# A gated MLP on one core: x transposed in bf16 groups inside five row chunks, gate and up weights read once per chunk, w_down loaded during the first stage

## The chip, the cores and the metric

One core of one Trainium2 chip. The metric is the device time of one execution in microseconds (us). "TensorE" is PE in the profile, "VectorE" DVE, "ScalarE" ACT, "GpSimd" POOL, "SyncE" SP. PSUM holds the tiles that TensorE writes to. PEld is the loading of a matmul's weights on TensorE. The granted clock (PEclk in the windows) is the share of its full clock that the profile shows for TensorE.

## The reference

```python
batch, seq_len, hidden_dim = 8, 1024, 1024        # M = 8192 rows, H = 1024
intermediate_dim = 4 * hidden_dim                 # I = 4096
def reference(x, w_gate, w_up, w_down):           # all float32
    gate = x @ w_gate
    up = x @ w_up
    gate = 0.5 * gate * (1 + np.tanh(np.sqrt(2 / np.pi) * (gate + 0.044715 * gate ** 3)))
    h = gate * up
    return (h @ w_down).astype(np.float32)
```

## The kernel before

The first stage transposes all of x with TensorE, then walks through 32 blocks of 128 columns of the gate and up weights; each block meets all 8192 rows, 512 at a time. The product h goes to DRAM. The second stage loads w_down and multiplies h by it. The lines that the argument touches:

```python
ident = const.tile([P, P], F32)
# --- first stage: P = 128, KH = 8, KI = 32, MT = 512
xt = xt_pool.tile([P, KH, M], BF16)                       # all of x, transposed: 128 KB a partition
for ms in range(NMS):                                     # 64 slices of 128 rows
    xs = stg.tile([P, H], F32, tag="xstage")
    nc.sync.dma_start(out=xs, in_=xf[ms * P:(ms + 1) * P, :])
    for ks in range(KH):
        pt = pst.tile([P, P], F32, tag="tp")              # two buffers
        nc.tensor.transpose(pt, xs[:, ks * P:(ks + 1) * P], ident)
        nc.vector.tensor_copy(out=xt[:, ks, ms * P:(ms + 1) * P], in_=pt)
for nb in range(KI):
    # ... wgf, wuf: 512 KB each by DMA; wgb, wub: their bf16 casts on GpSimd ...
    for mt in range(NMT):                                 # 16 row tiles of 512
        # ... 8 matmuls into gps, 8 into ups; gelu on ScalarE, product on VectorE, h to DRAM ...
# --- second stage, in pools of its own
wd = wd_pool.tile([P, KI, H], BF16)
for ko in range(KI):
    wdf = stg2.tile([P, H], F32, tag="wdf")               # two buffers
    nc.sync.dma_start(out=wdf, in_=wd_r[:, ko, :])
    nc.vector.tensor_copy(out=wd[:, ko, :], in_=wdf)
for mt in range(NMT):
    # ... hts: 4 MB of h; 8 accumulators (PSUM) of 32 matmuls each per tile, copied by ScalarE, written out ...
```

The program order is not the engine order: a scheduler interleaves the transposes with the first matmuls.

## Time and profile before

The median of the 13 runs of the kernel before is 2888.28 us; the span of the profiled run is 2886.6 us.

| stretch of the kernel before | time | its matmuls need | lost |
|---|---|---|---|
| first stage, to 1951.5 us | 1951.5 | 8192 x 215.83 ns = 1768.1 | 183 |
| second stage, to 2882.5 us | 931 | 4096 x 215.83 ns = 884.0 | 47 |
| tail | 4.1 | | 4 |

The spacing of 215.83 ns comes from the chain that ended last, in order of time (columns: start, length, what). One piece of the chain begins every 10.79 us and stands for 50 matmuls; one record in fifty is missing, so the line counts 49:

```profile
2066.07 10.74 PE ops L116 x49
2076.86 10.74 PE ops L116 x49
```

The page's chain shows how much of the span lies on TensorE:

```profile
PE 93%; DMA 3%; DVE 2%; issue 1%; SPq 0%; ACTq 0%; ACT 0%; DVEq 0%
```

The groups of instructions (columns: line, engine, operation, out<-in, shapes, count | busy us, mean ns of one | idle before, releaser) show the three kinds of matmul, the transposes (a matmul on L61) and their copies (L62):

```profile
L81 PE MATMUL gps<-xt,wgb 128*128 128x512 bf16 x4009 | 993.9, 384 | 4.2
...
L116 PE MATMUL ops<-wd,hts 128*128 128x512 bf16 x4014 | 887.1, 380 | 43.9 <-DVE wd L103 20.7
...
L61 PE MATMUL pt<-ident,xs 128*128 128x128 f32 x512 | 164.3, 358 | 46.7 <-DVE xt L62 28.3
...
L62 DVE CAST xt<-pt 128x128 bf16<-128x128 f32 x512 | 137.8, 290 | 90.0 <-PE pt L61 79.7
```

A matmul lasts 380 ns in its record, but a new one starts every 215.8 ns, as they overlap.

The stage windows (columns: window, its length, busy us and count of each engine, PEclk, DMA share, GB/s) show where the first stage loses its time:

```profile
50.00:100.00 50.00, 43.22 (x168) 22.77 (x170) 32.89 (x119) 1.79 (x3) 0.00 (x0) 0.76 0.48 160
100.00:150.00 50.00, 42.07 (x176) 21.79 (x176) 34.41 (x125) 2.39 (x4) 0.00 (x0) 0.84 0.51 168
240.00:300.00 60.00, 59.74 (x274) 27.20 (x278) 11.69 (x17) 10.75 (x18) 2.08 (x2) 1.00 0.24 74
```

From 50 to 150 us the granted clock is 0.76 to 0.84 and about 170 TensorE instructions, transposes among them, fit into 50 us; from 240 us on, 274 matmuls fit into 60.

### The profile page before, as it was taken

Reading aid. Unit: us, or ns where it says so; the run is one execution under the profiler, and the core shown is the slowest. Engines: PE = TensorE matmul, PEld = TensorE weight load, DVE = VectorE, ACT = ScalarE, POOL = GpSimd, SP = SyncE. Lnnn points to the kernel's source line nnn. Section 1 sums busy time; section 2 is a strip of 40 time slices with the busy share of each in tenths; the row PEclk is TensorE's granted clock in tenths of the full one; section 3 lists DMA queues with packets and bytes.
Section 4 is the critical chain, followed back from the end, with each engine's and each line's share of the span. In section 5 each row is a group of like instructions: output and inputs, shape, how many; then the busy total and the mean of one; then the engine's idle time right before and its main releaser. Section 6 shows DMA issues by size and latency. Waiting matters only on the chain.

```text
span 2886.6 us, 29837 instructions
## 1 busy us (share of the span) xinstructions
PE 2783.5 (96%) x12545; PEld 1278.0 (44%) x12800; DVE 510.7 (18%) x1056; ACT 381.2 (13%) x641; POOL 67.1 (2%) x70
## 2 busy tenths in 40 slices
PE   6889999999999999999999999995899999999999
PEld 3444444444444444444444444442344444444444
DVE  4663221112222222111222222111100000000000
ACT  0001111111111111111111111110000000000000
POOL 0000000000000000000000000000000000000000
PEclk8889999999999999999999999998999999999999
DMA  7452211211111121121121111118524224323321
GB/s 224 162 166 70 68 53 53 68 53 53 58 63 53 52 68 53 54 68 53 53 67 54 52 38 39 39 39 265 190 95 161 95 95 144 109 97 124 125 95 44
DMA packets 229254, 253.62 MB, mean 88 GB/s; under 512 B 12032, under 2 KB 208640, under 8 KB 229120
## 3 DMA queue, kind: packets, MB, share of 16 engines
q1 hardware_dynamic: 195840, 234.93, 24.3%
q10 hardware_dynamic: 33280, 16.78, 2.1%
q8 instruction: 100, 1.64, 0.2%
q14 instruction: 34, 0.28, 0.0%
HBM read 150.99 MB, written 100.66 MB: 87 GB/s over the span
## 4 chain that ended last, share of the span: by engine, by line
PE 93%; DMA 3%; DVE 2%; issue 1%; SPq 0%; ACTq 0%; ACT 0%; DVEq 0%
PE gps L81 31%; PE ups L84 30%; PE ops L116 29%; PE pt L61 3%; DMA wdf<-in_w_down_dram 3%; DVE xt L62 1%; DMA wuf<-in_w_up_dram 1%; SPq L102 0%; DVE wd L103 0%; DVE hsb L89 0%; DMA xs<-in_x_dram 0%; ACTq L73 0%; ACT osb L122 0%; SPq L90 0%; DVEq L89 0%
## 5 line engine op out<-in xcount | busy, mean ns | idle before, releaser
L81 PE MATMUL gps<-xt,wgb 128*128 128x512 bf16 x4009 | 993.9, 384 | 4.2
L84 PE MATMUL ups<-xt,wub 128*128 128x512 bf16 x4010 | 972.7, 379 | 4.2
L116 PE MATMUL ops<-wd,hts 128*128 128x512 bf16 x4014 | 887.1, 380 | 43.9 <-DVE wd L103 20.7
L116 PEld LDWEIGHTS <-hts 128*128 128x128 bf16 x4096 | 401.2, 98 | 529.7 <-issue 51.6
L81 PEld LDWEIGHTS <-wgb 128*128 128x128 bf16 x4096 | 407.0, 99 | 484.8 <-issue 15.0
L84 PEld LDWEIGHTS <-wub 128*128 128x128 bf16 x4096 | 404.3, 99 | 469.1
L89 DVE TENSOR_TENSOR hsb<-gsb,ups 128x512 bf16<-128x512 f32 x512 | 352.2, 688 | 1373.8 <-PE ups L84 1319.4
L87 ACT ACTIVATE gsb<-gps 128x512 f32<-128x512 f32 x512 | 305.7, 597 | 1623.5 <-PE gps L81 1553.6
L61 PE MATMUL pt<-ident,xs 128*128 128x128 f32 x512 | 164.3, 358 | 46.7 <-DVE xt L62 28.3
L122 ACT COPY osb<-ops 128x512 f32<-128x512 f32 x128 | 74.2, 588 | 858.5 <-PE ops L116 826.8
L62 DVE CAST xt<-pt 128x128 bf16<-128x128 f32 x512 | 137.8, 290 | 90.0 <-PE pt L61 79.7
L61 PEld LDWEIGHTS pt<-ident,xs 128*128 128x128 f32 x512 | 83.1, 163 | 120.4 <-DVE xt L62 93.4
L70 POOL CAST wgb<-wgf 128x1024 bf16<-128x1024 f32 x32 | 33.3, 1040 | 1692.2 <-PE gps L81 1475.3
L103 DVE CAST wd<-wdf 128x1024 bf16<-128x1024 f32 x32 | 22.2, 694 | 77.3 <-DMA wdf<-in_w_down_dram 77.3
L75 POOL CAST wub<-wuf 128x1024 bf16<-128x1024 f32 x32 | 33.3, 1040 | 27.0 <-PE ups L84 18.1
L87 ACT ACT_TABLE_LOAD x1 | 1.3, 1283 | 20.0 <-DMA wgf<-in_w_gate_dram 20.0
masks.py:199 POOL TENSOR_SCALAR_AFFINE_SELECT ident<-ident 128x128 f32<-128x128 f32 x1 | 0.3, 292 | 0.1
masks.py:197 POOL MEMSET ident<- 128x128 f32 x1 | 0.2, 204 | 0.3 <-POOLq L139 0.3
L139 POOL MEMSET const-float32-0.0<- 128x1 f32 x1 | 0.1, 98 | 0.2 <-issue 0.2
L139 POOL MEMSET const-bfloat16-1.0<- 128x1 bf16 x1 | 0.1, 102 | 0.0
L139 POOL MEMSET const-uint8-127<- 128x1 uint8 x1 | 0.1, 102 | 0.0
L139 POOL MEMSET const-float32-1.0<- 128x1 f32 x1 | 0.1, 98 | 0.0
## 6 DMA issues: line engine op xcount, KB each, us to landing
geglu_ht<-hsb SPq DMA_DIRECT2D x512, 128.0 KB, 1.7
hts<-geglu_ht SPq DMA_DIRECT2D x16, 4096.0 KB, 15.3
xs<-in_x_dram SPq DMA_DIRECT2D x64, 512.0 KB, 3.3
out_dram<-osb SPq DMA_DIRECT2D x64, 512.0 KB, 2.7
wuf<-in_w_up_dram ACTq DMA_DIRECT2D x32, 512.0 KB, 5.3
wgf<-in_w_gate_dram SPq DMA_DIRECT2D x32, 512.0 KB, 4.1
wdf<-in_w_down_dram SPq DMA_DIRECT2D x32, 512.0 KB, 4.2
```

Source lines behind the costliest of these rows:

```text
L61: nc.tensor.transpose(pt, xs[:, ks * P:(ks + 1) * P], ident)
L62: nc.vector.tensor_copy(out=xt[:, ks, ms * P:(ms + 1) * P], in_=pt)
L70: nc.gpsimd.tensor_copy(out=wgb, in_=wgf)
L75: nc.gpsimd.tensor_copy(out=wub, in_=wuf)
L81: nc.tensor.matmul(gps, wgb[:, ks, :], xt[:, ks, mt * MT:(mt + 1) * MT], start=(ks == 0), stop=(ks == KH - 1))
L84: nc.tensor.matmul(ups, wub[:, ks, :], xt[:, ks, mt * MT:(mt + 1) * MT], start=(ks == 0), stop=(ks == KH - 1))
L87: nc.scalar.activation(out=gsb, in_=gps, func=AF.Gelu_apprx_tanh)
L89: nc.vector.tensor_tensor(out=hsb, in0=gsb, in1=ups, op=mybir.AluOpType.mult)
L103: nc.vector.tensor_copy(out=wd[:, ko, :], in_=wdf)
L116: nc.tensor.matmul(ops, hts[:, ko, msub * P:(msub + 1) * P], wd[:, ko, dt * DT:(dt + 1) * DT], start=(ko == 0), stop=(ko == KI - 1),)
L122: nc.scalar.copy(out=osb[:, dt * DT:(dt + 1) * DT], in_=ops)
L139: nc = _bacc.Bacc("TRN2", target_bir_lowering=False, num_devices=1)
```

## The change

The intent: keep TensorE's matmuls dense from early on. x is transposed in bf16, eight 128x128 pieces to one PSUM tile with one VectorE copy; the rows are processed in five chunks, so that a chunk's transposes stand between matmuls of the chunk before; w_down is loaded during chunk 1, and the first tiles of h can be fetched before the first stage ends. The price: the gate and up weights are read five times.

```diff
+    wd = wd_pool.tile([P, KI, H], BF16)
+    def prep(xt, c, ms):
+        r0 = BASE[c] + ms * P
+        xs = stgx.tile([P, H], F32, tag="xstage", name="xs")
+        nc.sync.dma_start(out=xs, in_=xf[r0:r0 + P, :])
+        xb = stg.tile([P, H], BF16, tag="xstage_b", name="xb")
+        nc.gpsimd.tensor_copy(out=xb, in_=xs)
+        pt = pst.tile([P, KH, P], BF16, tag="tp", name="pt")
+        for ks in range(KH):
+            nc.tensor.transpose(pt[:, ks, :], xb[:, ks * P:(ks + 1) * P], ident)
+        nc.vector.tensor_copy(out=xt[:, :, ms * P:(ms + 1) * P], in_=pt)
+    CH = [1024, 2048, 2048, 2048, 1024]
+    for ms in range(CH[0] // P):
+        prep(xt_next, 0, ms)
+    for c in range(len(CH)):
+        xt = xt_next
         for nb in range(KI):
             # ... weights: loads and GpSimd casts as before, two staging buffers for three ...
+            if c == 1:
+                # ... wdf, one slice of w_down per block, cast on VectorE ...
-            for mt in range(NMT):
+            for mt in range(CH[c] // MT):
                 # ... matmuls as before; PSUM tiles gps and ups: two buffers for three ...
-                gsb = hp.tile([P, MT], F32, tag="gsb")
-                # ... gelu to gsb, product to hsb, one write of 512 columns ...
+                # ... gelu to hsb (bf16), product in place, two writes of 256 columns ...
+            if c + 1 < len(CH):
+                step = KI // (CH[c + 1] // P)
+                if nb % step == step - 1:
+                    prep(xt_next, c + 1, nb // step)
-    # ... second stage in its own pools: w_down loaded here, h in tiles of 512 rows, eight PSUM tiles ...
+    # ... second stage: h in tiles of 256 rows, two PSUM tiles, output written per 512 columns ...
```

## The prediction

> **What bounds it now.** TensorE. In the chain of waits, the second matmul stage advances by 10.79 us per 50 matmuls, 215.8 ns for each 512-column matmul, at granted clock 1.00. The Trainium skill ("TensorE: Matmul & The Clock Gate", Back-to-back issue gap) gives N/2.4 + 2.5 ns, 215.8 ns; the trace agrees. 12288 matmuls x 215.8 ns = 2652 us is a floor that the change doesn't touch. The span is 2886.6 us; 234.5 us is everything else. By the timeline and the stage windows:
> - The first stage ends at 1951.5 us, but its 8192 matmuls need 1768: **183 us** lost, nearly all before 240 us. There 512 fp32 transposes, each with its own PSUM tile and 290 ns VectorE copy, are interleaved singly with matmuls, the granted clock is 0.76 to 0.87, and the first matmul starts only at 26.4 us.
> - The second stage (1951.5 to 2882.5, 931 us) needs 884: **47 us** lost, where 32 weight slices (4.2 us to landing, then a 694 ns cast) are awaited.
> - Tail: 4 us.
>
> **What changes.**
> 1. Transposes: rows are cast to bf16 on GpSimd (about 1.04 us, as the weight casts there), eight bf16 transposes fill one PSUM tile, one VectorE copy empties it. By the instruction order, groups of eight stand between blocks of 64, 128 or 256 matmuls; only four groups precede the first matmul, eight the end of the start-up. The matmuls around them should keep the clock full. The 56 later groups stay on TensorE's path. Estimate: 0.9 us a group (the skill, same section, gives about 81 ns per sustained N=128 matmul; the trace's LDWEIGHTS is 98 ns, so about 100 ns a transpose, plus a switch), **50 us**.
> 2. Start-up: eight slices of x and two to four of each weight, at the 286 GB/s of the first 24 us, arrive by 20 to 25 us; minus 3.5 us of matmuls done meanwhile, **21 us** lost.
> 3. w_down is loaded and cast during chunk 1, and the first two tiles of h prefetched there: the 47 us go; **0 to 3 us** remain.
> 4. Added: the gate and up weights are read five times, 134 MB more. In the trace a 512 B packet takes 29.5 ns, 4 KB about 172 ns. Chunk 0 then needs weights 121 + h writes 30 + x 33 = 184 us of all 16 DMA engines in about 240 us: 77% busy. Weight loads run some two blocks (13.8 us) ahead and land in 4 to 5 us; so little waiting, **4 us** in all. Two instead of three PSUM buffers leave over 3 us of slack.
> 5. ScalarE and VectorE work per tile hardly changes and is off the path. Tail 4 us, launch 0.7.
>
> Sum: 2652 + 50 + 21 + 2 + 4 + 4 + 1 = 2734 us, 5.3% faster. Range 2712 to 2780. Chances: faster 0.95, same 0.04, slower 0.01.
>
> **What shows each step right or wrong.** The transposes' time per group of eight, about 0.9 us. Windows: clock near 1.00 after 30 us; chunk 0 (about 25 to 255 us) DMA share near 0.77, TensorE not waiting for GpSimd casts or weight DMAs. Timeline: first matmul about 18 us; no gap between stages; second stage about 884 us; matmul spacing still 215.8 ns.
>
> **What would make it wrong.** Transposes lowering the clock, or costing 150 ns or more each (+25 us); chunk 0 saturating the DMA engines, or in-order queues (weight loads in front of activations, casts in front of casts) making TensorE wait at block boundaries (+1 us per block would be +160 us).

## More of the kernel before

In the timeline of TensorE one sees the hand-over that slows the transposes: two small PSUM tiles go back and forth between TensorE and VectorE, and a pair takes 0.86 us (121.06 to 121.92).

```profile
121.06 0.69 PE L61 MATMUL pt<-ident,xs 128*128 128x128 f32 x2 [0.17 <-DVE xt L62]
121.92 0.69 PE L61 MATMUL pt<-ident,xs 128*128 128x128 f32 x2 [0.17 <-DVE xt L62]
```

## The result, and the profile after

The changed kernel takes 2709.31 us (median of 8 runs), the kernel before 2888.28 us. The ratio is 0.938, 95% interval 0.937 to 0.9389.

The direction and nearly all of the mechanism came as predicted, but 2709.3 lies 2.7 us below the range (2712 to 2780): the range missed.

The page after, groups of instructions and the chain:

```profile
PE 98%; DMA 1%; issue 1%; POOL 0%; SPq 0%; DVE 0%; ACT 0%; POOLq 0%; DVEq 0%; ACTq 0%
...
L112 PE MATMUL gps<-xt,wgb 128*128 128x512 bf16 x3999 | 961.9, 379 | 8.4 <-DVE xt L77 1.3
...
L76 PE MATMUL pt<-ident,xb 128*128 128x128 bf16 x512 | 41.2, 226 | 15.4 <-POOL xb L73 15.2
L76 PEld LDWEIGHTS <-xb 128*128 128x128 bf16 x512 | 35.2, 101 | 31.1 <-POOL xb L73 17.3
L77 DVE COPY xt<-pt 128x1024 bf16<-128x1024 bf16 x64 | 43.8, 685 | 22.5 <-PE pt L76 22.5
```

The transposes (L76) have a mean of 226 ns in their records, and their weight loads 101 ns. The timeline of TensorE in chunk 0 shows what they cost:

```profile
65.20 1.89 PE L115 MATMUL ups<-xt,wub 128*128 128x512 bf16 x8
66.93 0.61 PE L76 MATMUL pt<-ident,xb 128*128 128x128 bf16 x8
67.38 1.89 PE L112 MATMUL gps<-xt,wgb 128*128 128x512 bf16 x8
```

The group of eight starts at 66.93 us and the next matmul at 67.38: **0.45 us a group**, 55.6 ns a transpose, where 0.9 us was predicted. The 0.61 us in the line is the pipelined length, not the distance to the next start.

The stage windows after: the second is chunk 0, the third begins the second stage.

```profile
16.00:30.00 14.00, 10.94 (x72) 6.09 (x72) 4.75 (x7) 1.91 (x3) 8.72 (x9) 1.00 0.98 302
30.00:255.00 225.00, 223.79 (x1116) 105.97 (x1138) 54.25 (x81) 37.91 (x64) 83.40 (x81) 1.00 0.79 232
1820.00:2707.00 887.00, 879.48 (x4014) 400.45 (x4093) 0.47 (x1) 74.88 (x128) 0.00 (x0) 1.00 0.36 110
```

Chunk 0 has a DMA share of 0.79 (0.77 predicted), the clock is full, and TensorE is busy for 223.79 of 225 us. The start-up, in the timeline of TensorE:

```profile
19.65 1.01 PE L112 MATMUL gps<-xt,wgb 128*128 128x512 bf16 x2 [0.78 <-DVE xt L77]
...
28.05 1.89 PE L112 MATMUL gps<-xt,wgb 128*128 128x512 bf16 x8 [0.57 <-DVE xt L77]
```

The first matmul stands at 19.65 us, and dense matmuls begin at 28.05 us, when 16 of them (3.45 us) have been done: 24.6 us are lost.

All that TensorE waited for, by releaser (us in total, times, longest us):

```profile
PE pt L76 <- POOL xb L73: 15.2, 5, 5.8
PE gps L112 <- DVE xt L77: 1.3, 2, 0.8
PE gps L112 <- POOL wub L99: 1.2, 1, 1.2
PE ups L115 <- DVE hsb L119: 0.3, 1, 0.3
```

The first two lines are start-up. The third is one wait near 267 us, put down here to a GpSimd cast; the profile of a second run of the same kernel puts it down to ScalarE:

```profile
PE gps L112 <- ACT hsb L118: 1.2, 1, 1.2
```

That one fits: ScalarE had no free buffer for its output until a write of h landed, queued behind the 2 MB load of the first h tile, its activation ended at 267.88 us, and the matmul started at 267.93. So TensorE never waited for weights in the five passes, the start-up apart.

The terms, predicted and measured; the measured column adds up to the measured time within 0.1 us:

| term | predicted us | measured us | from |
|---|---|---|---|
| matmuls, 12288 | 2652 | 2652.1 | spacing 215.83 ns, unchanged |
| 56 later groups of transposes | 50 | 25.2 | 56 x 0.45 |
| start-up | 21 | 24.6 | 28.05 less 3.45 |
| handover to the second stage | 2 | 0 | the first of its matmuls starts at 1819.53, in step |
| waits on DMA and casts | 4 | 1.8 | two gaps that end at 267.93 and 277.02 us, by the distance of starts |
| tail | 4 | 3.5 | last matmul to the end of the span |
| launch | 1 | 2.0 | time of 2709.3 less span of 2707.3 |
| sum | 2734 | 2709.2 | |

The errors of the terms: -24.8, +3.6, -2, -2.2, -0.5 and +1. The groups account for the miss; that the other errors, +4.6 and -4.7 us in all, cancel is luck.

### The profile page after: what moved, and what is told of

It reads as the page before. It is cut to its first block, busy times and chain, and to the rows that moved or that the text cites. A ratio compares the mean times of both kernels' runs of the same rounds, so it can differ in the third digit from the quotient of the medians.

```text
span 2707.3 us, 32147 instructions
## 1 busy us (share of the span) xinstructions
PE 2672.3 (99%) x12547; PEld 1232.8 (46%) x12800; DVE 412.7 (15%) x608; ACT 381.7 (14%) x641; POOL 396.8 (15%) x390
## 4 chain that ended last, share of the span: by engine, by line
PE 98%; DMA 1%; issue 1%; POOL 0%; SPq 0%; DVE 0%; ACT 0%; POOLq 0%; DVEq 0%; ACTq 0%
PE ops L138 33%; PE gps L112 32%; PE ups L115 32%; PE pt L76 1%; DMA xs<-in_x_dram 0%; DMA geglu_ht<-hsb 0%; POOL xb L73 0%; SPq L123 0%; DVE hsb L119 0%; POOL wgb L94 0%; DVE xt L77 0%; ACT hsb L118 0%; ACT osb L145 0%; SPq L104 0%; SPq L71 0%
## 5 line engine op out<-in xcount | busy, mean ns | idle before, releaser
L112 PE MATMUL gps<-xt,wgb 128*128 128x512 bf16 x3999 | 961.9, 379 | 8.4 <-DVE xt L77 1.3
L115 PE MATMUL ups<-xt,wub 128*128 128x512 bf16 x4021 | 959.1, 379 | 3.3 <-DVE hsb L119 0.3
L119 DVE TENSOR_TENSOR hsb<-hsb,ups 128x512 bf16<-128x512 bf16 x512 | 352.0, 688 | 1318.4 <-PE ups L115 1051.7
L118 ACT ACTIVATE hsb<-gps 128x512 bf16<-128x512 f32 x512 | 305.6, 597 | 1490.6 <-PE gps L112 1438.0
L94 POOL CAST wgb<-wgf 128x1024 bf16<-128x1024 f32 x160 | 166.4, 1040 | 1287.9 <-PE gps L112 741.3
L99 POOL CAST wub<-wuf 128x1024 bf16<-128x1024 f32 x160 | 166.4, 1040 | 108.7 <-PE ups L115 101.2
L73 POOL CAST xb<-xs 128x1024 bf16<-128x1024 f32 x64 | 66.6, 1040 | 13.1 <-DMA xs<-in_x_dram 13.0
L76 PE MATMUL pt<-ident,xb 128*128 128x128 bf16 x512 | 41.2, 226 | 15.4 <-POOL xb L73 15.2
L76 PEld LDWEIGHTS <-xb 128*128 128x128 bf16 x512 | 35.2, 101 | 31.1 <-POOL xb L73 17.3
L77 DVE COPY xt<-pt 128x1024 bf16<-128x1024 bf16 x64 | 43.8, 685 | 22.5 <-PE pt L76 22.5
L118 ACT ACT_TABLE_LOAD x1 | 1.3, 1283 | 21.2 <-DMA wuf<-in_w_up_dram 21.2
```

The costliest lines, as they stand in the source:

```text
L73: nc.gpsimd.tensor_copy(out=xb, in_=xs)
L76: nc.tensor.transpose(pt[:, ks, :], xb[:, ks * P:(ks + 1) * P], ident)
L77: nc.vector.tensor_copy(out=xt[:, :, ms * P:(ms + 1) * P], in_=pt)
L94: nc.gpsimd.tensor_copy(out=wgb, in_=wgf)
L99: nc.gpsimd.tensor_copy(out=wub, in_=wuf)
L112: nc.tensor.matmul(gps, wgb[:, ks, :], xt[:, ks, mo:mo + MT], start=(ks == 0), stop=(ks == KH - 1))
```

## The experiments

All outputs are right. A name that starts with a_ is a variant of the changed kernel, with b_ of the kernel before. The changed kernel was run again twice as a reference: 2708.69 us and 2709.53 us.

> The changed kernel again, unaltered, as the reference for its variants on this chip: about 2709 us, 0.938 of the kernel before.

> The changed kernel again, unaltered, as the reference for the runs beside it on this chip: about 2709 us.

### Is it the price of a group? The transposes done twice

```diff
-        for ks in range(KH):
-            nc.tensor.transpose(pt[:, ks, :], xb[:, ks * P:(ks + 1) * P], ident)
+        for rep in range(2):
+            for ks in range(KH):
+                nc.tensor.transpose(pt[:, ks, :], xb[:, ks * P:(ks + 1) * P], ident)
```

> Every group of eight bf16 transposes is done twice into the same PSUM tile (result unchanged). Theory: a group costs TensorE 0.45 us, 128/2.4 + 2.5 ns per transpose with the weight loads hidden behind it, and all of it lies on the critical path. Then 56 groups add 25 us, and the eight start-up groups up to 6 us more: 2734 to 2741 us, with groups of sixteen taking about 0.90 us between matmuls. First rival: a group really costs about 0.9 us as predicted and something else hid half of it: +50 us or more, 2759 us and up. Second rival: the groups run in slack of TensorE: +5 us or less.

Measured: 2740.37 us against 2708.69 for the reference beside it, 31.7 us more (expected 25 to 31). The timeline of TensorE:

```profile
70.27 1.89 PE L116 MATMUL ups<-xt,wub 128*128 128x512 bf16 x8
72.00 1.06 PE L77 MATMUL pt<-ident,xb 128*128 128x128 bf16 x16
72.89 1.89 PE L113 MATMUL gps<-xt,wgb 128*128 128x512 bf16 x8
```

Sixteen transposes take 0.89 us, from 72.00 to 72.89; a doubled group follows its predecessor by 14.70 us (72.00 to 86.70), where the undoubled kernel has 14.26 us (66.93 to 81.19 by the same pattern, 66.44 to 80.70 in the reference's run). So a further group costs 0.445 us, and 56 of them 24.9 us. About 4.4 us more come from the start-up: dense matmuls begin at 30.70 in place of 28.05 us, and the first sixteen of them still run slowly and take 5.14 us in place of 3.45. Against the reference's own run, where dense matmuls begin at 27.56 us, the start-up makes 4.8 us; the waits near 277 to 304 us are 0.9 us longer in all, and the profiled execution (2739.3) lay 1.1 us under the median, which makes up the rest. Had a group cost 0.9 us with half of it hidden, the run would have been at 2759 us or more; had the groups run in slack, it would not have moved. Both rivals fall.

### Is bf16 what makes the groups cheap? fp32 transposes in the changed kernel

```diff
-        xb = stg.tile([P, H], BF16, tag="xstage_b", name="xb")
-        nc.gpsimd.tensor_copy(out=xb, in_=xs)
-        pt = pst.tile([P, KH, P], BF16, tag="tp", name="pt")
-        for ks in range(KH): ...
+        for g in range(2):
+            pt = pst.tile([P, 4, P], F32, tag="tp", name="pt")
+            for k in range(4):
+                ks = g * 4 + k
+                nc.tensor.transpose(pt[:, k, :], xs[:, ks * P:(ks + 1) * P], ident)
+            nc.vector.tensor_copy(out=xt[:, g * 4:g * 4 + 4, ms * P:(ms + 1) * P], in_=pt)
```

> The changed kernel with fp32 transposes straight from the loaded rows (no cast), in two groups of four, each with one PSUM bank and one VectorE copy. The kernel before, at half rate, shows about 0.21 us for one fp32 transpose beside a matmul, so about 0.11 us at full rate. Theory (element type only doubles the streaming time, placement keeps the clock): a pair of groups costs about 0.9 us in place of 0.45, +25 us, up to +45 if the longer fp32 weight load isn't hidden; 2734 to 2755 us, matmuls still 215.8 ns apart. Rival (fp32 transposes themselves bring the clock down, as the low clock of the kernel before might suggest): matmuls 427 ns apart for microseconds after each group, +100 us or more.

Measured: 2737.51 us, 28.8 us more than the reference, inside the range of the theory.

```profile
70.91 1.04 PE L76 MATMUL pt<-ident,xs 128*128 128x128 f32 x8
71.79 1.89 PE L112 MATMUL gps<-xt,wgb 128*128 128x512 bf16 x8
```

Eight fp32 transposes take 0.88 us, 110 ns each, almost what sixteen bf16 ones take; the clock stays full (0.998 on average) and the next matmuls run at their usual spacing. An fp32 transpose thus costs twice a bf16 one here, and groups of eight between blocks of matmuls do not bring the clock down. The rival falls. The 0.43 us more for 56 pairs of groups make 24 of the 28.8 us; a longer start-up (3.6) and longer waits (1.2) are nearly all of the rest.

### Where did the 183 us of the first stage come from? The kernel before with other transposes

Three variants of the kernel before leave the single pass over the weights and the late w_down as they are.

One: bf16, but still one PSUM tile and one copy for each transpose.

```diff
+            xb = stg.tile([P, H], BF16, tag="xstage_b")
+            nc.gpsimd.tensor_copy(out=xb, in_=xs)
             for ks in range(KH):
-                pt = pst.tile([P, P], F32, tag="tp")
-                nc.tensor.transpose(pt, xs[:, ks * P:(ks + 1) * P], ident)
+                pt = pst.tile([P, P], BF16, tag="tp")
+                nc.tensor.transpose(pt, xb[:, ks * P:(ks + 1) * P], ident)
```

> The kernel before with rows cast to bf16 on GpSimd and bf16 transposes, but still one PSUM tile and one VectorE copy per transpose. In the kernel before a pair of transposes takes 0.86 us where no matmul stands between, of which TensorE streams little: TensorE and VectorE hand two small PSUM tiles back and forth. Theory (the hand-over is the cost, not the element type): little is gained, 15 to 50 us, 2840 to 2875 us, and the clock stays below 0.9 in the first 240 us. Rival (fp32 transposes are the cost): most of the 183 us goes, 2780 us or less.

Measured: 2839.63 us against 2887.40 for the kernel before beside it: 47.8 us gained, at the edge of what the theory allowed. The clock was 0.81 to 0.87 from 24 to 200 us, as expected, but 1.00 from then on, as the transposes were through at 187 us. Part of this gain may be hand-over too: with bf16 the VectorE copy of a tile takes 222 ns on average in place of 290.

Two: fp32, four to a PSUM bank and one copy for four (the loop over g and k of the fp32 experiment above, in the kernel before).

> The kernel before with its fp32 transposes in groups of four that share one PSUM bank and one VectorE copy. Theory (the hand-over is the cost): 128 hand-overs in place of 512, about 90 us of VectorE copies in place of 148, so 80 to 120 us gained, 2770 to 2810 us, and a clock of 0.9 or more after about 60 us. Rival (fp32 is the cost): a gain of 20 us or less.

Measured: 2809.34 us, 78.1 us gained: the bottom edge of the theory, far from the rival; the clock was 1.00 and 0.97 in the two windows from 50 to 150 us, as expected. Grouping alone brings more than the element type alone.

Three: bf16 and eight to a tile, as in the changed kernel.

> The kernel before with the transposes as in the changed kernel (bf16, eight to a PSUM tile, one copy), everything else as before: all of x is loaded and transposed up front, w_down between the stages. Theory: what is left of the 183 us is the load of x: 33.5 MB take 88 us of all engines (8192 packets of 172 ns) while the first weight block has 55 us of matmuls, so 45 to 70 us stay lost in the first stage, 2750 to 2775 us, and the chunks of the changed kernel account for the rest of its first-stage gain (about 40 us). If the chunks matter little, 2735 us or less.

Measured: 2815.84 us, 71.6 us gained. I expected 112 us or more. The three windows from 100 to 150 us, one for each variant in this order:

```profile
100.00:150.00 50.00, 40.45 (x220) 21.45 (x223) 32.66 (x152) 2.99 (x5) 18.76 (x18) 0.81 0.63 200
```

```profile
100.00:150.00 50.00, 43.58 (x266) 29.49 (x272) 32.54 (x50) 2.99 (x5) 0.00 (x0) 0.97 0.82 260
```

```profile
100.00:150.00 50.00, 32.38 (x214) 20.67 (x217) 18.96 (x28) 1.79 (x3) 20.87 (x21) 0.62 0.75 247
```

The grouped variants are through with the transposes at 144.3 us (fp32) and 139.8 us (bf16), and in both the last row slice is issued to DMA only at 138.9 and 132.6 us: the load of x is the limit, at 247 to 282 GB/s. In bf16 TensorE mostly waits for the row casts, and these for the rows; this is all its waiting on GpSimd and theirs on DMA:

```profile
POOL xb L60 <- DMA xs<-in_x_dram: 52.1, 54, 3.4
...
PE pt L63 <- POOL xb L60: 49.1, 36, 9.1
```

My expectation had priced 33.5 MB of x at 88 us, at 172 ns for a packet of 4 KB and as if the engines did nothing else and never paused (the packets of x in the kernel before took 197 ns on average); it took about 137 us, with only the 55 us of the first weight block to cover it. In bf16 TensorE is busy for only 32.38 of the 50 us in that window and its clock is 0.62, which may be why the fp32 groups, which keep it busier, come out 6 us ahead; no run settles that.

In these variants the first stage ends at 1902.6, 1871.8 and 1878.7 us (start of the last VectorE product), so 135, 104 and 111 us of the 183 stay lost. In the changed kernel the first stage ends at 1819.8 us, 51.7 us over its matmuls. I put the difference down to the chunks: only 4.2 MB of x must come before the first chunk's 32 weight blocks can run. No run changes the chunks alone (the changed kernel also has fewer buffers and loads w_down in this stage); the run with a first chunk twice as long, below, loses 8.6 us more at the start, which points the same way. The size also depends on the kind of transpose: with fp32 groups the same step, from 1871.8 to 1848.2 us, is 24 us and not 59, as the dearer groups then stand on TensorE's path.

### What was loading w_down late worth?

```diff
-            if c == 1:
-                wdf = stg.tile([P, KH, P], F32, tag="wgf", name="wdf")
-                # ... one slice, cast on VectorE ...
+    for ko in range(KI):           # after the loops of the first stage
+        wdf = stg.tile([P, KH, P], F32, tag="wgf", name="wdf")
+        # ... the same load and cast ...
     for mt in range(NMT2):
```

> The changed kernel with w_down loaded after the first stage's loops in place of during chunk 1 (the scheduler still starts about ten of its 32 slices earlier, as their place in SBUF is free). Theory: TensorE must wait for the slices again, with only two PSUM accumulators to take up slices as they come where the kernel before had eight: +40 to +90 us, 2750 to 2800 us, all of it at the start of the second stage. Rival: the 47 us of the kernel before came from the tiles of h and not from w_down: +10 us or less.

Measured: 2763.13 us, about 54 us more than the changed kernel. The waits of TensorE:

```profile
PE ops L138 <- DVE wd L128: 35.4, 24, 2.4
```

The second stage starts at 1823.7 us and its last matmuls end near 2758: 934 us, 50 more than its 884. Of these 35.4 are plain waits for slices. The rest is slow running between waits, at a granted clock of 0.59 from 1823 to 1887 us, with matmuls 0.38 to 0.43 us apart, as here (two matmuls, 0.38 us from start to start):

```profile
1839.49 1.01 PE L138 MATMUL ops<-wd,hts 128*128 128x512 bf16 x2 [1.72 <-DVE wd L128]
```

So w_down loaded late is enough by itself to cost about as much as was lost before, and the rival (tiles of h alone) falls. That w_down made all of the 47 us in the kernel before is not shown, and its own trace speaks against it. These are the casts of the first two slices of w_down there, and TensorE's first matmuls of the second stage:

```profile
1955.34 0.69 DVE L103 CAST wd<-wdf 128x1024 bf16<-128x1024 f32 x1 [3.04 <-DMA wdf<-in_w_down_dram]
1957.08 0.69 DVE L103 CAST wd<-wdf 128x1024 bf16<-128x1024 f32 x1 [1.04 <-DMA wdf<-in_w_down_dram]
...
1970.34 4.86 PE L116 MATMUL ops<-wd,hts 128*128 128x512 bf16 x14 [18.82 <-issue]
```

Two slices were ready by 1957.8 us, yet TensorE stood still until 1970.34: the first tile of h (4 MB), issued at 1953.22, landed 16.9 us later, at 1970.1. The third and fourth slices, issued while it was under way, landed only at 1971.4 and 1972.7. So the tiles of h have a share in the 47 us (TensorE stood for 12 us with two slices ready), and the changed kernel moved both loads forward. How the 47 us divide is open; that the 50 us here come so near to them is in part chance, with two accumulators in place of eight.

### What limits the start-up?

Even chunks:

```diff
-    CH = [1024, 2048, 2048, 2048, 1024]
+    CH = [2048, 2048, 2048, 2048]
```

> The changed kernel with four chunks of 2048 rows in place of 1024, 2048, 2048, 2048, 1024. Sixteen slices of x (8.4 MB) must now come before the first weight block is through, which has 13.8 us of matmuls in place of 6.9. At about 300 GB/s, x and the first weights take about 33 us; so the start-up loses about 25 to 35 us in place of 24.6, of which eight more groups of transposes (3.6 us) leave the later path. Theory (start-up is bytes ahead of the first matmuls): 2706 to 2716 us. If the small chunks at both ends matter more than that, 2725 us or more; fewer weight reads (four in place of five) should by themselves change nothing, as TensorE doesn't wait for them.

Measured: 2717.68 us, 8.2 us more than the reference beside it (2709.53), just above the range of the theory. Dense matmuls begin at 43.60 us, after 48 of them (10.4 us): 33.2 us lost, 8.6 more than before, less 3.6 for eight groups that leave the later path. Another 1.6 us are a longer wait for ScalarE (2.8 us in place of 1.2). The other 1.6 us I did not trace.

The loads in another order (eight row slices in the idle h buffers, so that none waits for a staging buffer):

```diff
+    xa = [hp2.tile([P, 4, H], F32, tag="hts", name="xa") for _ in range(2)]
+    for ms in range(4):
+        nc.sync.dma_start(out=xa[0][:, ms, :], in_=xf[ms * P:(ms + 1) * P, :])
+    first = [loadw(0, nc.sync)]          # the first gate and up slices, on the same queue
+    for ms in range(4):
+        nc.sync.dma_start(out=xa[1][:, ms, :], in_=xf[(4 + ms) * P:(5 + ms) * P, :])
+    first.append(loadw(1, nc.sync))
```

> The changed kernel with its start-up reordered: the eight row slices of chunk 0 are staged in the two idle h buffers, so that none waits for a buffer; four of them, then the first gate and up weight slices, then the other four are issued on one queue. If the 24.6 us lost before steady matmuls are the wait for x behind weight loads, the first matmul comes at about 12 us in place of 19.7 and the steady state at 18 to 22 us in place of 28: 6 to 10 us faster than the control, 2699 to 2703 us. If the start-up is limited by the bytes themselves or by the cold clock, no change within 2 us.

Measured: 2705.55 us, 3.1 us less than the reference; half of the least that was hoped. The first matmul came at 14.70 us, dense matmuls at 23.25. GpSimd shows why the first isn't earlier: the fourth row cast stood behind a weight cast that waited for its DMA.

```profile
7.65 1.04 POOL L74 CAST xb<-xa 128x1024 bf16<-128x1024 f32 x1 [0.92 <-DMA xa<-in_x_dram]
10.80 1.04 POOL L112 CAST wgb<-wgf 128x1024 bf16<-128x1024 f32 x1 [2.11 <-DMA wgf<-in_w_gate_dram]
11.79 1.04 POOL L74 CAST xb<-xa 128x1024 bf16<-128x1024 f32 x1
```

Two more steps: the first two weight casts go to ScalarE, and the tiles of h get five buffers in place of three (rows two in place of three, for space).

```diff
-            nc.gpsimd.tensor_copy(out=wgb, in_=wgf)        # and wub in the same way
+            (nc.scalar.copy if c == 0 and nb == 0 else nc.gpsimd.tensor_copy)(out=wgb, in_=wgf)
-    stgx = ...(tc.tile_pool(name="p1_xs", bufs=3))         hp = ...(name="p1_h", bufs=3)
+    stgx = ...(tc.tile_pool(name="p1_xs", bufs=2))         hp = ...(name="p1_h", bufs=5)
```

> The reordered start-up, with two more things: the first block's two weight casts go to ScalarE, so that no row cast on GpSimd stands behind a cast that waits for its weights (in the reordered start-up the fourth row cast began at 11.8 us for that reason), and five buffers for the tiles of h in place of three (two for rows in place of three), so that writes of h stuck behind the two big loads of h don't hold up ScalarE (the 1.8 us wait near 263 us). Expected: first matmul at 11 to 12.5 us in place of 14.7, steady matmuls at 20 to 22 us in place of 23.3, no wait near 263 us: 2 to 5 us below the reordered start-up, 2700 to 2704 us. If only bytes limit it, 2704 to 2706 us.

Measured: 2703.48 us, 6.1 us less than its reference, the best but one of all runs. The first matmul comes at 11.50 us, dense matmuls at 21.94. But the fifth row cast starts only at 13.45 us, released by its DMA, so bytes now set the pace. And the wait at the handover did not go, it moved:

```profile
PE ups L131 <- DVE hsb L135: 2.2, 1, 2.2
```

```profile
270.07 0.69 DVE L121 CAST wd<-wdf 128x1024 bf16<-128x1024 f32 x1 [8.67 <-DMA wdf<-in_w_down_dram]
270.69 1.28 DVE L135 TENSOR_TENSOR hsb<-hsb,ups 128x512 bf16<-128x512 bf16 x2
```

The cast of a w_down slice waited 8.67 us for a load that stands in the queue with the load of an h tile, and the products that follow it in VectorE's program ran only after it, from 270.69 us. So more h buffers were the wrong cure.

At last, 22 matmuls of zeros between the first groups, to bring the clock up early:

```diff
+        if ms in (0, 2, 3):
+            for _ in range({0: 10, 2: 4, 3: 8}[ms]):
+                nc.tensor.matmul(warm, ident, zero, start=True, stop=True)
         prep(xt_next, 0, ms, xs=xa[ms // 4][:, ms % 4, :])
```

> As the run before, with 22 matmuls of zeros into an unused PSUM tile between the first groups of transposes, so that TensorE's clock is up before the first real matmul (in the reordered start-up matmuls stood 427 ns apart until 19 us). If the slow first matmuls lie on the path, 1 to 3 us less than the run before; if TensorE is waiting for x anyway, no change, and up to 2 us more if the zeros get in the way.

Measured: 2703.21 us against 2703.48: no change. The first transposes then ran at full rate, but TensorE waited 3.51 us for a row cast before the fifth group, and by 18 us the matmuls were slow again. So a full clock early brings nothing while TensorE is short of x; what a clock held full to the end of the start-up would bring, the run does not show.

## Why the prediction was right or wrong

- **What bounds the kernel: right.** The matmul spacing stayed at 215.83 ns; the floor of 2652 us holds in both kernels.
- **Step 1, "Estimate: 0.9 us a group ... 50 us": the step that failed.** A group costs 0.45 us, all of them 25.2 us. Two inputs were wrong. The weight load's 98 ns was taken as the price of a transpose, as if it occupied TensorE; it is the length of a record that overlaps its neighbours, and 55.6 ns from start to start is all that shows. And the prediction named N/2.4 + 2.5 ns for the 512-column matmul, confirmed by the trace, but took another figure of the same section of the Trainium skill (81 ns, raised to 100 for the weight load) for 128 columns; the same formula gives 55.8 ns there. The switch that it added does not show either: sixteen transposes take twice as long as eight. That the groups lie on TensorE's path, and that the matmuls around them keep their clock, was right; doubling the groups added 0.445 us for each.
- **Step 2, start-up of 21 us: right in kind, 24.6 measured.** It is x behind buffers, casts and bytes, as the reordered loads show (3.1 and 6.1 us back).
- **Step 3, the 47 us of the second stage go: right.** No time is lost between the stages. The prediction put the 47 us down to the slices of w_down alone; loading w_down late brings 50 us back, but in the kernel before the first tile of h was awaited too.
- **Step 4, five reads of the weights nearly free: right.** DMA share 0.79, and no wait for weights after the start-up. The 1.8 us of gaps come from the first h tiles' loads, which hold up writes of h and slices of w_down in the queue.
- **The range: too narrow below.** It stopped at 2712, though the formula that the prediction itself quoted gave 25 us for the groups.
- **What the prediction left out:** it said that the 183 us would go, not what each part of the change was worth. Grouped bf16 transposes alone recover 72 us; the step to the changed kernel, most likely the chunks, which shorten what must be loaded before TensorE can run, the next 59 (first stage ending at 1878.7 against 1819.8 us).

## What to carry to other kernels

Price a small instruction on a pipelined engine by the distance between starts, or by a formula that the same trace confirms at another size, never by the length of its records; if an estimate mixes both, widen the range to hold both. When transposes slow a matmul kernel, first batch them into one PSUM tile and one copy, then ask what must be loaded before the engine has work: here the step to the chunked kernel was worth nearly as much (59 us) as the batching (72 us). Reading the weights five times cost nothing here after the start-up, with the DMA engines under 80% busy and the loads running ahead.

## What the Trainium skill lacked or had wrong

- "TensorE: Matmul & The Clock Gate", Back-to-back issue gap: it gives a sustained roofline of about 81 ns per matmul at N=128 and 131 ns at N=512 for streams of weight load and matmul. Here every matmul has its own weights, and the spacing is 55.6 ns at 128 columns (eight transposes in 0.45 us) and 215.83 ns at 512. The formula on the same page that it calls isolated, N/2.4 + 2.5 ns, fits both.
- The same page, LDWEIGHTS: it gives P/1.2 ns, 107 ns for 128 columns. The records here last 98 to 101 ns, near that, but start every 55.6 ns in a group of transposes, so this length is not what a stream pays; the section doesn't say so, though Part 2 of the page does say that the next weights load while a matmul runs.
- The same page, Part 4 (PE-mode transpose): it gives about 275 to 390 ns for a 128x128 bf16 transpose. In a group between matmuls a transpose takes 219 ns (median of the records) and costs 55.6 ns. Of fp32 its table of terms says only that the transpose mode is four times faster, without a time: 110 ns here.
- The same page, Part 4, says that the clock gate does not open for transposes. Groups of eight, and sixteen, between blocks of 64 matmuls kept full rate here (0.45 and 0.89 us). And in the run with doubled transposes the clock came up on transposes alone: they are all that TensorE had run when, after 4.7 us of them almost without a pause from 16.51 us on, their spacing fell from 107 to 56 ns at 21.2 us, before the first matmul at 21.54. The run with fp32 transposes, too, records a full clock at 12.07 us, when TensorE had run nothing but transposes. The sentence does not hold for these two runs.
- I found no page that says so: the granted clock of a profile window can read 1.00 before full rate is reached. In the first 16 us of the changed kernel the window reads 1.00, but a group of eight transposes lasts 1.03 us there and 0.61 us later; the trace has no record of the clock before 22.8 us.
